# Moving the first w_down burst one pair of w_up tiles forward and pausing three times instead of twice

## The chip, the cores and the metric

The kernel runs on one core of a Trainium2 chip. The metric is the device time in microseconds of one execution, as a median over runs. The engines are named as in the profile: PE (matmuls), PEld (PE's weight loads), DVE (VectorE), ACT (ScalarE), POOL (GpSimd), SP (the engine that issues most of the DMAs).

## The reference: what is computed

One decoder layer on 256 positions of 1024 channels, float32. A first half (three kinds of attention, gates, an output projection and a residual) is followed by the gated channel mixer, which is where the change lies:

```python
    x = x + merged @ w_o

    h2 = rmsnorm(x, ln2)
    u = causal_dwconv(h2 @ w_up, conv_w, conv_b)
    a, b = jnp.split(u, 2, axis=-1)
    return x + (jax.nn.silu(a) * b) @ w_down
```

Here h2 is 256 x 1024, w_up is 1024 x 5632 (two halves of 2816 columns, for a and b), the convolution reaches over three positions per channel, and w_down is 2816 x 1024. A last rmsnorm follows. The inner width of 2816 is 22 blocks of 128 (NF = 22).

## The kernel before

**Weights.** All weights come as a stream of pieces of 128 x 1024 floats, in the order in which PE uses them. Each piece is loaded by SP into one of five `raw` buffers, ACT copies it in a rounded form to `whi` (line 113), and DVE subtracts the two to get the rest, `wlo` (line 120). A product is then three matmuls: hi by hi, hi by lo, lo by hi. `piece()` takes the next piece of the stream; `ahead()` prepares one more piece, some eight pieces ahead of the one in use. There are ten buffers each for `whi` and `wlo`.

**The channel mixer.** A loop over j = 0 to 21 makes one block of 128 inner channels at a time. It takes two pieces of w_up: `up(j, 0, u[0])` for the a half and `up(j, 1, u[1])` for the b half, 24 matmuls of 256 columns each, into the PSUM tiles called s (two of them, for even j) or pt and o (for odd j). In this document u0, u1, u2 are these pairs of w_up tiles. The matmuls read `h2T`, which has the name oT in the profile. `conv_of` takes a tile from PSUM to DVE (`v`, line 838), does the convolution on ACT and DVE (lines 841 to 845) and calls `ahead()` once. Silu and a product give `pr` (line 908); ACT rounds it to `ah` (line 914), DVE makes the rest `al` (line 915). These two are what w_down multiplies, and they have six buffers.

**The w_down bursts.** A row block d of w_down is one piece, and `down(d, parts)` is a burst of 12 matmuls of 512 columns, whose stationary operands are `ah` and `al` of block d. In this document d0, d1, ... are these bursts. A list decides after which pair which burst comes: `downs_after()` gives for each j a burst or none, and in the list the bursts go in order. The last four blocks (TAIL = 4) come after the loop. The stream of pieces in DRAM is laid out from the same list, so each piece still comes in the order of its use.

```python
        d = downs[j]
        if d is not None:
            parts = piece(0)
            ahead()
        nc.scalar.activation(hi, pr, AF.Copy)
        nc.vector.tensor_sub(lo, pr, hi.bitcast(F32))
        mid[j] = (hi, lo)
        if d is not None:
            down(d, parts)
```

So in a pair j with a burst, DVE and ACT prepare three pieces, and otherwise two. On DVE and ACT the third one stands between `pr` and `ah`, `al` of the same j. Engines run their own instructions strictly in the order in which the code issues them, and wait for each other by semaphores.

**Before u0.** The second rmsnorm needs the sum of squares of the whole x. Its factor goes to all partitions as `row2`, by matmuls (line 290) in the middle of u0 and a copy on ACT. Every `v` multiplies by `row2`, so DVE cannot begin with u0's tiles before that.

Of the kernel before, what the change touches and what calls it, by code (L numbers as in the profile page):

```python
# [37 lines left out]
          fours=(37.46, 53.0, 68.5, 83.5), mm=18.0)  # L38
DL = dict(pos=1.0, sq0=0.5, sq1=0.53, rs=1.0, row=1.0, q=1.98, g1=0.47, g2=0.64, s1=1.0, s2=1.43,
          s3=1.0, b=0.8, qk=1.9, half=2.0, ex=2.6, sc=1.3, fl=1.2, va=1.9, vh=0.9)  # L40
PAUSES = (9, 16)


def downs_after():

    out, d = [], 0
    for j in range(NF):
        if j >= 2 and j not in PAUSES:
            out.append(d)
            d += 1  # L50
        else:
            out.append(None)
    assert d == NF - TAIL
    return out
# [89 lines left out]
def hybrid_kernel(ctx: ExitStack, tc: tile.TileContext, x, head, ln_f, w_main, w_v1, w_v2, table,  # L144
# [742 lines left out]
    for r in (64, 0):  # L887
# [4 lines left out]
        if r:  # L892
            ml.tile([P, 48], F32, name="gap")

    downs = downs_after()
    for j in range(NF):
        u = up_banks(j)
# [164 lines left out]
```

## Time and profile before

| | |
|---|---|
| median of 3 runs | 382.51 us (382.28 to 382.6) |
| the profiled execution's own time | 381.96 us |
| its span in the trace | 380.2 us |
| PE busy | 372.1 us (98%) |
| DVE busy | 287.7 us (76%) |
| ACT busy | 230.3 us (61%) |
| granted clock of TensorE, mean | 0.997 |

The span runs from the first to the last instruction of the program; the execution's own time has some 1.8 us around it. Busy times are those of instructions that the engine works on. Matmuls are pipelined, and the duration of one overlaps the next, so the distance between two starts is their pace.

### The profile page before, as it was taken

Reading aid. Unit: us, or ns where it says so; the run is one execution under the profiler, and the core shown is the slowest. Engines: PE = TensorE matmul, PEld = TensorE weight load, DVE = VectorE, ACT = ScalarE, POOL = GpSimd, SP = SyncE. Lnnn points to the kernel's source line nnn. Section 1 sums busy time; section 2 is a strip of 40 time slices with the busy share of each in tenths; the row PEclk is TensorE's granted clock in tenths of the full one; section 3 lists DMA queues with packets and bytes.
Section 4 is the critical chain, followed back from the end, with each engine's and each line's share of the span. In section 5 each row is a group of like instructions: output and inputs, shape, how many; then the busy total and the mean of one; then the engine's idle time right before and its main releaser. Section 6 shows DMA issues by size and latency. Waiting matters only on the chain.

```text
span 380.2 us, 6522 instructions
## 1 busy us (share of the span) xinstructions
PE 372.1 (98%) x2470; PEld 334.6 (88%) x2470; DVE 287.7 (76%) x541; ACT 230.3 (61%) x398; POOL 5.0 (1%) x15
## 2 busy tenths in 40 slices
PE   8999999999999999999999999999999999999992
PEld 8999998787878788888899999999999999999982
DVE  4687876575757537967788999888987888888745
ACT  5875574547647694337587667556655656565433
POOL 1020000000000000000000000000000000000000
PEclk9999999999999999999999999999999999999998
DMA  7989964443442627435636567665566555563002
GB/s 254 400 286 345 334 187 167 139 159 132 166 165 90 218 92 267 161 117 166 243 98 233 203 218 238 208 208 181 174 216 193 197 183 205 171 218 110 2 0 110
DMA packets 20530, 70.86 MB, mean 186 GB/s; under 512 B 2278, under 2 KB 2708, under 8 KB 20500
## 3 DMA queue, kind: packets, MB, share of 16 engines
q1 hardware_dynamic: 19764, 68.11, 52.9%
q0 software_dynamic: 592, 2.12, 1.7%
q8 instruction: 19, 0.31, 0.3%
q10 hardware_dynamic: 144, 0.23, 0.2%
q14 instruction: 11, 0.09, 0.1%
HBM read 69.38 MB, written 1.07 MB: 185 GB/s over the span
## 4 chain that ended last, share of the span: by engine, by line
PE 96%; DMA 1%; DVE 1%; ACT 0%; SPq 0%; issue 0%; DVEq 0%
PE acc L244 16%; PE s L833 16%; PE acc L246 16%; PE acc L245 16%; PE pt L833 8%; PE o L833 8%; PE acc L390 7%; PE s L618 2%; DMA begin<-in_head 1%; PE pt L390 1%; PE o L390 1%; PE s L565 1%; PE s L607 1%; PE s L302 0%; PE pt L565 0%; PE pt L772 0%
## 5 line engine op out<-in xcount | busy, mean ns | idle before, releaser
L120 DVE TENSOR_TENSOR wlo<-raw,whi 128x1024 fp32r<-128x1024 f32 (+3 forms) x122 | 144.8, 1201 | 14.2 <-ACT whi L113 14.1
L113 ACT ACTIVATE whi<-raw 128x1024 fp32r<-128x1024 f32 (+3 forms) x122 | 124.1, 1038 | 42.8 <-PE acc L245 20.6
L833 PE MATMUL s<-oT,whi 128*128 128x256 f32 x352 | 62.5, 278 | 0.0
L244 PE MATMUL acc<-whi,hThi 128*128 128x512 f32 (+2 forms) x160 | 61.4, 384 | 0.0
L245 PE MATMUL acc<-whi,hTlo 128*128 128x512 f32 (+2 forms) x160 | 59.9, 374 | 0.0
L246 PE MATMUL acc<-wlo,hThi 128*128 128x512 f32 (+2 forms) x160 | 59.8, 374 | 0.0
L833 PEld LDWEIGHTS s<-oT,whi 128*128 128x128 f32 x352 | 54.1, 188 | 0.4
L833 PE MATMUL s<-oT,wlo 128*128 128x256 f32 x176 | 48.7, 277 | 0.0
L841 ACT ACTIVATE ya<-v,cv 128x256 f32<-128x256 f32 x22 | 13.3, 602 | 41.5 <-DVE v L838 41.5
L244 PEld LDWEIGHTS acc<-whi,hThi 128*128 128x128 f32 x160 | 30.0, 188 | 6.1 <-issue 1.3
L246 PEld LDWEIGHTS acc<-wlo,hThi 128*128 128x128 f32 x160 | 30.0, 188 | 5.2
L245 PEld LDWEIGHTS acc<-whi,hTlo 128*128 128x128 f32 x160 | 30.1, 188 | 4.7 <-DVE hTlo L296 0.2
L246 PE MATMUL acc<-wlo,ah 128*128 128x512 f32 (+1 forms) x88 | 34.1, 388 | 0.0
L244 PE MATMUL acc<-whi,ah 128*128 128x512 f32 (+1 forms) x88 | 34.0, 387 | 0.0
L245 PE MATMUL acc<-whi,al 128*128 128x512 f32 (+1 forms) x88 | 33.9, 385 | 0.0
L833 PEld LDWEIGHTS s<-oT,wlo 128*128 128x128 f32 x176 | 33.2, 188 | 0.4
L833 PE MATMUL pt<-oT,whi 128*128 128x256 f32 x176 | 32.1, 278 | 0.0
L833 PE MATMUL o<-oT,whi 128*128 128x256 f32 x176 | 31.8, 277 | 0.0
L833 PEld LDWEIGHTS pt<-oT,whi 128*128 128x128 f32 x176 | 27.4, 188 | 0.4
L833 PEld LDWEIGHTS o<-oT,whi 128*128 128x128 f32 x176 | 27.3, 188 | 0.0
L833 PE MATMUL pt<-oT,wlo 128*128 128x256 f32 x88 | 24.4, 277 | 0.0
L833 PE MATMUL o<-oT,wlo 128*128 128x256 f32 x88 | 24.3, 276 | 0.0
(236 smaller groups left out, 635.9 us busy)
## 6 DMA issues: line engine op xcount, KB each, us to landing
raw<-in_w_main SPq DMA_DIRECT2D x115, 512.0 KB, 3.5
begin<-in_head SPq DMA_DIRECT2D x6, 384.0 KB, 6.5
raw<-in_w_v SPq DMA_DIRECT2D x4, 384.0 KB, 3.9
xt<-in_x SPq DMA_DIRECT2D x2, 512.0 KB, 8.1
G<-rowsd POOLq DMA_DIRECT2D x1, 1024.0 KB, 14.3
raw<-in_w_v SPq DMA_DIRECT2D x2, 390.0 KB, 8.0
out_y<-xt SPq DMA_DIRECT2D x2, 288.0 KB, 2.2
begin<-in_head SPq DMA_DIRECT2D x2, 256.0 KB, 3.6
```

The source lines that it names most:

```text
L113: self.nc.scalar.activation(self.parts[i][0][:, cs], self.raw[i][:, cs], AF.Copy)
L120: self.nc.vector.tensor_sub(lo[:, cs], self.raw[i][:, cs], hi[:, cs].bitcast(F32))
L244: nc.tensor.matmul(o, lh, rh, start=start, stop=False, **kw)
L245: nc.tensor.matmul(o, ll, rh, start=False, stop=False, **kw)
L246: nc.tensor.matmul(o, lh, rl, start=False, stop=stop, **kw)
L390: nc.tensor.matmul(o, w[:, kk, cs], hT[h][:, k, :], start=first, stop=last, skip_group_check=True)
L565: nc.tensor.matmul(sc[2 * i + e][:, lo:lo + m], q[h, qi, qs], k[h, ki, 0:m], start=True, stop=True)
L607: nc.tensor.transpose(pts[h][:, i * P:(i + 1) * P], L[:, h, i * P:(i + 1) * P], ident)
L618: nc.tensor.matmul(os[i][e * HD:(e + 1) * HD, cs], v[t][:, vi, e, :], p[:, S:ROWS] if t else p[:, 0:S], start=t == 0, stop=t == 1, **kw)
L833: nc.tensor.matmul(u, w, h2T[h][:, k, :], start=k == 0 and i == 0, stop=k == KD - 1 and i == 2)
L841: nc.scalar.activation(y, v, AF.Identity, scale=w[2], bias=w[3])
```

## The change

```diff
-PAUSES = (9, 16)
+PAUSES = (8, 13, 18)
...
-        if j >= 2 and j not in PAUSES:
+        if j >= 1 and j not in PAUSES:
             out.append(d)
             d += 1
```

Before, d0 follows u2, and the pairs 9 and 16 have no burst behind them: a burst stands two pairs behind its block up to j = 8, three up to j = 15 and four up to j = 21. Now d0 follows u1, and the pairs 8, 13 and 18 have none: a burst stands one pair behind its block up to j = 7, two up to j = 12, three up to j = 17 and four up to j = 21. There are 18 bursts in the loop in both.

On PE, from the last matmul of u1 on, this stood before (`o` is u1's second tile, `s_2230` and `s_2231` are u2, `ah_2145` and `al_2146` are block 0, so the rows of line 244 to 246 are d0, and `pt` is u3):

```order
L833 MATMUL o<-oT,whi 128x256
L833 MATMUL s_2230<-oT,whi 128x256 [waits DVE_49]
...
L833 MATMUL s_2231<-oT,whi 128x256 [waits DVE_49,Activation_49]
...
L244 MATMUL acc<-whi,ah_2145 128x512 [waits Activation_49]
L245 MATMUL acc<-whi,al_2146 128x512 [waits DVE_49]
L246 MATMUL acc<-wlo,ah_2145 128x512
...
L833 MATMUL pt<-oT,whi 128x256 [waits DVE_49]
```

At the same place PE now has this (`s_2252` and `s_2253` are u2, `ah_2226` and `al_2227` are block 1, so the last two rows begin d1):

```order
L833 MATMUL o<-oT,whi 128x256
L244 MATMUL acc<-whi,ah_2145 128x512 [waits Activation_49]
L245 MATMUL acc<-whi,al_2146 128x512 [waits DVE_49]
L246 MATMUL acc<-wlo,ah_2145 128x512
...
L833 MATMUL s_2252<-oT,whi 128x256
...
L833 MATMUL s_2253<-oT,whi 128x256
...
L244 MATMUL acc<-whi,ah_2226 128x512 [waits Activation_49]
L245 MATMUL acc<-whi,al_2227 128x512 [waits DVE_49]
```

The 12 matmuls of d0, the first of which waits for `ah` and the second for `al` of block 0, have moved ahead of the 48 of u2.

On DVE nothing moves up to `pr` of block 1. Behind it, this is the first place where the two differ (`v<-s_2230` is the first work on u2's tiles):

```order
 L845 SCALAR_TENSOR_TENSOR yb<-v,cv,yb 128x254
 L908 TENSOR_TENSOR pr<-ya,yb 128x256
+L120 TENSOR_TENSOR wlo<-raw,whi 128x1024
 L915 TENSOR_TENSOR al_2227<-pr,ah_2226 128x256
-L838 TENSOR_TENSOR v<-s_2230,row_2074 128x256
```

Pair 1 now has a burst, so a third `wlo` stands ahead of `al` of block 1. What makes `al` of block 0 stands ahead of this, in the same rows as before.

## Rows read from the trace of the kernel before

**Rows 1.** The page, parts 1 and 4: busy time of each engine; the chain that ended last

```profile
PE 372.1 (98%) x2470; PEld 334.6 (88%) x2470; DVE 287.7 (76%) x541; ACT 230.3 (61%) x398; POOL 5.0 (1%) x15
PE 96%; DMA 1%; DVE 1%; ACT 0%; SPq 0%; issue 0%; DVEq 0%
```

**Rows 2.** The waits of PE's matmuls, whole span: us in total, times, longest

```profile
PE s L212 <- DVE warm L209: 1.1, 1, 1.1
PE s L618 <- DVE nm L577: 0.2, 1, 0.2
```

**Rows 3.** The waits of all engines, 212 to 366 us

```profile
DVE v L838 <- PE s L833: 8.2, 14, 1.1
```

**Rows 4.** The chain that ended last, in order of time: start us, us, what

```profile
203.48 5.65 PE s L833 x48
...
220.12 5.47 PE s L833 x48
...
266.66 5.44 PE s L833 x48
```

**Rows 5.** Timeline of PE, u2 to d1: start us, us, instruction

```profile
203.32 0.28 PE L833 MATMUL s<-oT,whi 128*128 128x256 f32 x1
...
208.97 0.40 PE L244 MATMUL acc<-whi,ah 128*128 128x512 f32 x1
...
211.77 0.28 PE L833 MATMUL pt<-oT,whi 128*128 128x256 f32 x1
...
217.21 0.39 PE L244 MATMUL acc<-whi,ah 128*128 128x512 f32 x1
...
219.96 0.28 PE L833 MATMUL s<-oT,whi 128*128 128x256 f32 x1
```

**Rows 6.** Timeline of DVE, blocks 0 to 2; in brackets idle before, and releaser

```profile
204.57 0.43 DVE L908 TENSOR_TENSOR pr<-ya,yb 128x256 f32<-128x256 f32 x1
205.47 0.43 DVE L915 TENSOR_TENSOR al<-pr,ah 128x256 fp32r<-128x256 f32 x1 [0.48 <-ACT ah L914]
205.82 0.42 DVE L838 TENSOR_TENSOR v<-pt,row 128x256 f32<-128x256 f32 x1
...
210.69 0.43 DVE L908 TENSOR_TENSOR pr<-ya,yb 128x256 f32<-128x256 f32 x1
...
211.95 0.42 DVE L838 TENSOR_TENSOR v<-s,row 128x256 f32<-128x256 f32 x1
...
216.82 0.43 DVE L908 TENSOR_TENSOR pr<-ya,yb 128x256 f32<-128x256 f32 x1
217.17 1.22 DVE L120 TENSOR_TENSOR wlo<-raw,whi 128x1024 fp32r<-128x1024 f32 x1
218.30 0.42 DVE L915 TENSOR_TENSOR al<-pr,ah 128x256 fp32r<-128x256 f32 x1
218.64 0.42 DVE L838 TENSOR_TENSOR v<-pt,row 128x256 f32<-128x256 f32 x1
```

**Rows 7.** Timeline of ACT, block 0 and the third piece of pair 2

```profile
205.03 0.42 ACT L914 ACTIVATE ah<-pr 128x256 fp32r<-128x256 f32 x1 [0.92 <-DVE pr L908]
...
215.32 2.00 ACT L113 ACTIVATE whi<-raw 128x1024 fp32r<-128x1024 f32 x2
```

**Rows 8.** Timeline, 7.8 to 10 us: a DVE result that PE waits for

```profile
8.50 0.69 DVE L120 TENSOR_TENSOR wlo<-begin,whi 128x512 fp32r<-128x512 f32 x1
...
9.25 0.38 PE L390 MATMUL pt<-hThi,wlo 128*128 128x256 f32 x1
```

**Rows 9.** The page, part 6: DMA issues of the weights, KB each, us to landing

```profile
raw<-in_w_main SPq DMA_DIRECT2D x115, 512.0 KB, 3.5
```

**Rows 10.** Timeline of PE: the first matmuls, eight of the same shape, the last matmul

```profile
1.10 3.35 PE L212 MATMUL s<-warm 128*128 128x128 f32 x14 [1.10 <-DVE warm L209]
...
172.49 1.03 PE L302 MATMUL s<-ident,G 128*128 128x128 f32 x8
...
373.21 0.28 PE L246 MATMUL s<-wlo,ah 128*128 128x256 f32 x1
```

**Rows 11.** Windows at the end: us, busy us of PE, PEld, DVE, ACT, POOL, PEclk, DMA share, GB/s

```profile
377.00:378.00 1.00, 0.00 (x0) 0.00 (x0) 0.00 (x0) 0.00 (x0) 0.00 (x0) 1.00 0.81 315
378.00:379.00 1.00, 0.00 (x0) 0.00 (x0) 0.00 (x0) 0.00 (x0) 0.00 (x0) 0.50 0.56 210
```

## The prediction, made before the changed kernel ran

> **What bounds the kernel now.** I read the page first. PE is busy for 98% of the span, and the chain that ended last is PE for 96% of it [rows 1]. So the time is PE's queue from end to end, and an edit costs or gains what it does to that queue. The next question is whether PE waits anywhere. The view of waits, asked for PE alone, has two entries over the whole span, 1.1 us at the start and 0.2 us in the attention part [rows 2]. In the channel mixer, where the change lies, there is none: PE goes from tile to tile without a gap, and it is DVE that waits there for PE, 14 times for the s tiles alone [rows 3].
>
> What is left are differences in PE's pace, which the chain in order of time shows. A pair of w_up tiles (48 matmuls) takes 5.65 us in u2, but 5.47 us later where a burst stands ahead of it, and 5.44 us behind a pair without a burst [rows 4]. The timeline of PE gives the bursts: d0 runs from 208.97 to 211.77, 2.80 us; d1 from 217.21 to 219.96, 2.75 us; between them u3 takes 5.44 us [rows 5]. So up to d0's end PE runs at a slightly slower pace, and from u3 on at the faster one. The trace does not say why; it shows that the switch came at the first change from a burst of 512 columns to w_up.
>
> The third view is the timeline of DVE and ACT at the place to which d0 moves. There DVE is far behind PE. PE leaves u1 and starts u2 at 203.32 [rows 5]. At that time `pr` of block 0 is not made yet: DVE makes it at 204.57, ACT `ah` from 205.03 to 205.45, DVE `al` from 205.47 to 205.90 [rows 6, 7]. The order of before hides this lag behind u2, 5.65 us of PE work. That is the point on which the prediction turns.
>
> **The change part by part.**
>
> *d0 behind u1.* PE reaches d0 at 203.32. Its first matmul needs `ah` of block 0, its second `al`. All that leads to these two stands in the same order on DVE and ACT as before, so their times hold. From the end of a DVE result to the matmul that waits for it I take 0.06 us: the `wlo` that began at 8.50 and took 0.69 us ended at 9.19, the matmul started at 9.25 [rows 8]. So the first matmul starts at about 205.45 + 0.06 = 205.51, and the second at 205.90 + 0.06 = 205.96, since its result is later than the first matmul needs. From the second on, 11 starts at 2.75 / 12 = 0.229 us bring d0's end to 205.96 + 2.52 = 208.48. The wait itself is 203.32 to 205.51, plus some 0.2 us between the first and the second matmul: about 2.4 us. The nearest row for the release is one of three in the trace's first microseconds; nothing for the release would make the sum smaller by 0.06.
>
> *What the pause gives back.* If the faster pace comes with the first burst, u2 takes 5.47 instead of 5.65 and d1 2.75, and u3, which now follows a burst, 5.47. The end of d1 and u3 together: 208.48 + 5.47 + 2.75 + 5.47 = 222.17. Before, the same four blocks (u2, d0, u3, d1) ended at 219.96 [rows 5]. That is +2.21 us. If the slow pace stays until d1 is over, d0 ends at 205.96 + 11 x 0.233 = 208.53, and with 5.65, 2.80 and 5.44 the four end at 222.42, +2.46 us. Of the two I take the faster pace, because the one switch in the trace came at the first burst; the other is the upper end.
>
> *d1 and later bursts, one pair behind their block.* In pair 1 a third `whi` and `wlo` now stand ahead of `al` of block 1. From `pr` to the end of `al` a pair with a third piece takes 218.30 + 0.42 - 216.82 = 1.90 us; ACT's two `whi` in such a pair (2.00 us) begin well ahead of `pr` [rows 6, 7]. `pr` of block 1 stands at 210.69, so `al` of block 1 is ready at 212.59. PE reaches d1 at 208.48 + 5.47 = 213.95, so there is a margin of 1.3 us. From then on it grows: DVE takes 218.64 - 211.95 = 6.69 us for a pair with three pieces [rows 6], PE takes 5.47 + 2.75 = 8.22. Cost nothing; if DVE lost more than 1.3 us in pair 1, PE would wait for the excess.
>
> *Three pauses instead of two, at other places.* In a pair without a burst PE needs 5.44 us and DVE 211.95 - 205.82 = 6.13 us [rows 4, 6], so DVE falls back by 0.7 us in each, and makes up 8.22 - 6.69 = 1.5 us in the next pair with a burst. Behind each pause a burst stands one pair further from its block, which is more room than the 0.7 us. The cover is the time in which DVE waits for PE [rows 3]; without it, 0.7 us per pause, and even that is smaller than the pair of room. Cost nothing. The changes from a burst to w_up, each 0.03 us (5.47 against 5.44), are 17 instead of 16; two of the 17 are in the sum above, so -0.03 remains against the 16 of before.
>
> *The pieces' order.* As many pieces, 115 loads of 512 KB, land in 3.5 us each [rows 9]. The fifth piece of the mixer's stream, once u2's first, is now w_down's first block. It is wanted at 203.32, as the fifth was before, and the next ones later than before, so preparation that was in time stays so. Cost nothing.
>
> *What a pause may do to PE's clock.* The last matmul of the program starts at 373.21, and the granted clock is still 1.00 in the window from 377 to 378, where no engine has an instruction; in the next window it is 0.50 [rows 10, 11]. The new wait is shorter than that stretch, so I add nothing. The Trainium skill, "TensorE: Matmul & The Clock Gate", section "HAM oscillation — how this bites in real kernels", says that a wait in which PE idles can throttle it and make the next matmuls run cold; by the rows of this case the sum gains nothing by that, by the rule, where it applied, it would gain about 1.6 us (the third rival works this out from rows).
>
> *Sum.* +2.21 - 0.03 = +2.2 us on PE, which has no later wait that could absorb it [rows 2]. The profiled execution took 381.96, which gives 384.2 for it; the median of the runs is 0.55 above the profiled one, 382.51 + 2.2 = **384.7 us**. Of no change a measurement of this kernel can tell about 0.2%, 0.77 us, so this would be slower, by 0.6%.
>
> **The rivals.**
>
> *First, not slower: no wait at d0.* If `al` of block 0 were ready at about 203.5, only the pace would change: u2 5.47 instead of 5.65, d0 2.75 instead of 2.80, together -0.23, 382.3 us. It decides at 203.5 + 0.06: `al` would have to come 2.4 us earlier than its row shows. For it speaks that DVE sat idle 0.48 us just ahead of `al`, and that a chain with three engines need not fall the same each time. Against it: what is ahead of `al` is untouched, and the idle time is far smaller than 2.4 us [rows 6]. That the burst doesn't move is excluded by the order on PE. Chance 0.05, of which 0.01 for faster by over 0.2%.
>
> *Second, d1 waits too.* The third piece in pair 1 comes late, because its raw load or its buffers are not free in time when DVE and ACT ask for it one pair earlier. The price beyond the margin: one `whi` and one `wlo` in a row (1.0 + 1.2 us [rows 6, 7]) less the margin of 1.3, so 0.9 us, 385.6 us; less if only part of it is late. For it: the third piece is the one that is new at this place. Against it: landing takes 3.5 us, and raw buffers run five pieces ahead. Chance 0.06.
>
> *Third, the clock falls in the wait.* The first 14 matmuls of the program, 128 columns each, took 3.35 us, eight of the same shape later 1.03 [rows 10], so at full pace the 14 would have taken 1.8 us: a start from rest cost some 1.6 us. If the wait for `ah` cost that again, it gives 384.7 + 1.6 = 386.3 us. Against it stand the windows at the end. It decides at a granted clock below 1.00 behind 203 us. Chance 0.04. It is the case that the page named above warns of.
>
> **How the numbers follow.** The forecast has a chance of 0.85. Its own bounds are +2.1 to +2.5 us, with the spread of the three runs around their median (-0.23, +0.09) 384.4 to 385.1. The second rival's smaller cases and a release that takes longer lie above this, up to 385.5; below, a DVE chain that is 0.2 us quicker gives 384.2. The range of **384.2 to 385.5** leaves out the first and the third rival and the far end of the second. Faster 0.01, same 0.04, slower 0.95.
>
> **What would show it.** In the profile of the changed kernel PE's waits should have a new entry at line 244 or 245 (or at their weight loads), released by ACT `ah` and DVE `al`, 2 to 2.5 us in all, near 203.3; `al` of block 0 should end at about 205.9 as before; u2 should take 5.47 us; d1 should start without a wait near 214; from there on every block should stand about 2.2 us later than before, with the same lengths, to the end. The prediction is wrong if `al` of block 0 comes earlier than its row here shows, if PE makes up time behind d1, or if u2 and d1 wait.

## The result and the profile after

The changed kernel takes 384.84 us (median of 5 executions, 384.8 to 386.74) against 382.28 us (median of 5, 382.14 to 382.6) in the same measurement. The ratio is 1.0075 with a 95% interval of 1.0063 to 1.0087: slower by 2.4 to 3.3 us. The profiled execution took 384.83 us, with a span of 383.1 us.

The page of the changed kernel, parts 1, 2 and 4: busy time of each engine, PE over the span in 40 slices, and the chain that ended last. They answer to [rows 1].

```profile
PE 372.0 (97%) x2470; PEld 333.9 (87%) x2470; DVE 288.1 (75%) x541; ACT 230.7 (60%) x398; POOL 5.0 (1%) x15
...
PE   7999999999999999999997999999999999999992
...
PE 94%; DVE 2%; DMA 1%; ACT 1%; issue 0%; SPq 0%; DVEq 0%
```

PE's busy time is that of before (372.0 against 372.1 us), and its share has fallen: the added time is time in which PE has nothing to do. The chain passes through DVE and ACT for a stretch. The slice of PE with a 7 in mid-span is from 201 to 211 us.

The waits of PE's matmuls over the whole span, which answer to [rows 2] (us in total, times, longest):

```profile
PE acc L244 <- ACT ah L914: 2.0, 1, 2.0
PE s L212 <- DVE warm L209: 1.1, 1, 1.1
PE pt L390 <- ACT whi L113: 0.5, 1, 0.5
PE o L390 <- ACT whi L113: 0.3, 1, 0.3
PE pt L390 <- DVE wlo L120: 0.2, 1, 0.2
PE s L618 <- DVE nm L577: 0.2, 1, 0.2
```

The first row is new and is the wait of d0 for `ah` of block 0. The three rows of line 390 lie in the first microseconds of the program, at the first weights; they belong to how this one execution began, and will be needed below to read the other times.

Timeline of PE at the end of u1, in d0 and at the start of u2, d1, u3 and d2, which answers to [rows 5]:

```profile
203.80 0.28 PE L833 MATMUL o<-oT,whi 128*128 128x256 f32 x1
206.09 0.49 PE L244 MATMUL acc<-whi,ah 128*128 128x512 f32 x1 [2.01 <-ACT ah L914]
206.55 0.50 PE L245 MATMUL acc<-whi,al 128*128 128x512 f32 x1
206.88 0.39 PE L246 MATMUL acc<-wlo,ah 128*128 128x512 f32 x1
...
209.18 0.28 PE L833 MATMUL s<-oT,whi 128*128 128x256 f32 x1
...
214.64 0.39 PE L244 MATMUL acc<-whi,ah 128*128 128x512 f32 x1
...
217.39 0.28 PE L833 MATMUL pt<-oT,whi 128*128 128x256 f32 x1
...
222.85 0.39 PE L244 MATMUL acc<-whi,ah 128*128 128x512 f32 x1
```

And that of DVE, which answers to [rows 6]:

```profile
205.16 0.42 DVE L908 TENSOR_TENSOR pr<-ya,yb 128x256 f32<-128x256 f32 x1
206.07 0.43 DVE L915 TENSOR_TENSOR al<-pr,ah 128x256 fp32r<-128x256 f32 x1 [0.48 <-ACT ah L914]
...
212.77 0.42 DVE L915 TENSOR_TENSOR al<-pr,ah 128x256 fp32r<-128x256 f32 x1
```

`pr` and `al` of block 0 stand 0.59 and 0.60 us later than in [rows 6], with the same distance between them. So this execution is 0.60 us late before the change has any effect (0.62 us at the first matmul of line 244: 18.88 against 18.26 before), and 0.60 is to be taken off every time here. The last u1 matmul starts at 203.80, the first of d0 at 206.09, the second, which needs `al`, at 206.55. d0 is over at 209.18; u2 takes 5.46 us, and d1 starts at 214.64, without a wait: `al` of block 1 ended at 213.19.

Last, the end of PE's work, which answers to [rows 10]:

```profile
376.08 0.28 PE L246 MATMUL s<-wlo,ah 128*128 128x256 f32 x1
```

That is 2.87 us later than the 373.21 of before. Without the 0.60 of the start it is 2.27 us. Nearly the same stands at the end of u3, where u2, d0, u3 and d1 are all done: 222.85 less 0.60, against 219.96 before, is 2.29 us.

### The profile page after: what moved, and what is told of

Its sections match the earlier page's. It is cut to its first block, busy times and chain, and to the rows that moved or that the text cites. A ratio compares the mean times of both kernels' runs of the same rounds, so it can differ in the third digit from the quotient of the medians.

```text
span 383.1 us, 6510 instructions
## 1 busy us (share of the span) xinstructions
PE 372.0 (97%) x2470; PEld 333.9 (87%) x2470; DVE 288.1 (75%) x541; ACT 230.7 (60%) x398; POOL 5.0 (1%) x15
## 4 chain that ended last, share of the span: by engine, by line
PE 94%; DVE 2%; DMA 1%; ACT 1%; issue 0%; SPq 0%; DVEq 0%
PE acc L244 16%; PE s L833 16%; PE acc L245 15%; PE acc L246 15%; PE pt L833 7%; PE o L833 7%; PE acc L390 7%; PE s L618 2%; DMA begin<-in_head 1%; PE pt L390 1%; PE o L390 1%; PE s L565 1%; PE s L607 1%; DVE wlo L120 0%; PE s L302 0%; PE pt L565 0%
```

## The experiments

Each was measured beside the kernel before on the same chip, in three series: the first with the four runs up to the shorter wait, the second with the two repeats, the first filling and the first delay of `al`, the third with the rest. The three series ran on three chips. With each run stands the number of timed executions.

**Is it the move or the pauses?** The move alone keeps d0 behind u1, and then pauses at pair 2, after which list and lags are those of before:

```diff
-PAUSES = (8, 13, 18)
+PAUSES = (2, 9, 16)
```

> d0 behind u1 as in the change, then a pause at pair 2 and the pauses at 9 and 16 of before: the move alone. Theory (the wait for block 0 at d0 is the whole cost): PE waits some 2.3 us at d0, +2.2 to +2.3 us from there, about 384.5 to 384.8 us, as the change. Rival (the pauses at other places, or the bursts one pair behind their blocks later on, carry a part): clearly less than the change, down to 382.3 us.

Measured: 386.28 us (5 executions, 386.04 to 386.85) against 382.39 of before (29 executions), ratio 1.0093 (1.0075 to 1.0111). This is slower than the change itself, and neither the theory nor the rival had expected that. The profile has the same wait of 2.01 us. But d0 took 4.44 us from its first matmul (205.96) to that of u2 (210.40), where it took 3.09 in the profile of the change, and the windows show why (columns as in [rows 11]):

```profile
204.00:205.00 1.00, 0.00 (x0) 0.00 (x0) 0.96 (x3) 0.57 (x1) 0.00 (x0) 1.00 0.74 291
205.00:206.00 1.00, 0.04 (x1) 0.04 (x1) 0.48 (x3) 0.42 (x1) 0.00 (x0) 0.96 0.83 229
206.00:207.00 1.00, 1.00 (x2) 0.75 (x3) 1.00 (x3) 0.26 (x1) 0.00 (x0) 0.50 0.73 287
...
209.00:210.00 1.00, 1.00 (x5) 0.77 (x5) 1.00 (x2) 1.00 (x3) 0.00 (x0) 0.84 0.90 311
```

The granted clock fell to 0.50, 1.2 GHz, as the wait ended, and came back during 209 to 210 us. That is the third rival of the prediction, which had been given 0.04.

The pauses alone keep d0 behind u2, as before:

```diff
-PAUSES = (9, 16)
+PAUSES = (13, 18)
```

> d0 behind u2 as before, pauses at 13 and 18 instead of 9 and 16: bursts two pairs behind their blocks up to pair 12. Theory: PE waits nowhere in the mixer, the time of before, 382.1 to 382.6 us. Rival (the later pauses cost): above 382.8 us, with a wait of PE behind pair 13.

Measured: 382.37 us (12 executions) against 382.39, ratio 0.9998 (0.9986 to 1.001). PE has no wait in the mixer. These other places for the pauses cost nothing.

**Is it the wait?** Here d0 stands between the two tiles of u2, one tile later than in the change; the list is that of before (left out of this cut: the later d0 of pair 2 is taken away, and its piece is laid one tile earlier in the stream):

```diff
+        if j == 2:
+            down(0, piece(0))
         if j:
             up(j, 1, u[1])
...
```

> The list of before, but d0 stands between the two tiles of u2, one tile of PE work (2.8 us) later than in the change. Theory: PE gets there at about 206.2, al of block 0 is ready at 205.9, so no wait to speak of (0 to 0.2 us) and the time of before, 382.0 to 382.5 us; the faster pace begins one tile earlier, -0.1 us. Rival (an earlier d0 costs by the other order of pieces, or by a burst between two w_up tiles, not by the wait): 383 us or more.

Measured: 382.31 us (12 executions) against 382.39, ratio 0.9993 (0.9982 to 1.0003). PE's waits again have no entry in the mixer. So this earlier d0 costs nothing, nor does a burst between two tiles; in the change it is one tile too early. The timeline of PE shows the pace change with the burst:

```profile
203.94 0.28 PE L833 MATMUL s<-oT,whi 128*128 128x256 f32 x1
...
206.77 0.40 PE L244 MATMUL acc<-whi,ah 128*128 128x512 f32 x1
...
209.56 0.28 PE L833 MATMUL s<-oT,whi 128*128 128x256 f32 x1
...
212.29 0.28 PE L833 MATMUL pt<-oT,whi 128*128 128x256 f32 x1
```

u2's first tile, ahead of d0, takes 2.83 us, its second, behind it, 2.73.

Then a shorter wait: the change with one `ahead()`, so one `whi` and one `wlo`, moved from `up_first` to behind `al` of block 0.

```diff
         for f in finish:
             f()
-        ahead()
...
         nc.vector.tensor_sub(lo, pr, hi.bitcast(F32))
+        if j == 0:
+            ahead()
```

> The change, with the preparation of one piece (one whi, one wlo) moved from ahead of u0's first v to behind al of block 0. Theory: ah and al of block 0 come 0.9 to 1.0 us earlier, the wait shrinks by as much, and the time by as much: 383.8 to 384.0 us. Rival (the cost is not the wait for block 0): the time of the change, 384.8 us, or more.

Measured: 383.61 us (12 executions, 383.31 to 384.01) against 382.39, ratio 1.0026 (1.0016 to 1.0037). The wait in the profile is 0.95 us shorter, as expected. The time is 1.2 us less than that of the change in its first measurement, which is another series, and a little under the 383.8 that were expected at least; the traces, compared below, give 0.93. In all 12 executions the mean clock was 0.994 to 0.998:

```profile
205.16 0.50 PE L244 MATMUL acc<-whi,ah 128*128 128x512 f32 x1 [1.06 <-ACT ah L913]
```

**What does the clock add?** The changed kernel and the move alone were each run once more.

> The changed kernel once more. Theory (wait of 2.3 us, and in some executions the granted clock falls to 0.50 behind the wait, which costs 1.3 to 1.9 us more): most executions at 384.8 us, one in five or so near 386.5. Rival (the move alone is slower than the change for another reason, its pause at pair 2): all executions near 384.8 us.

> The move alone once more. Theory (wait plus clock): executions at two levels, about 384.7 us where the clock stays and 386.0 to 386.8 us where it falls. Rival (its pause at pair 2 costs by itself): all at 386.0 us or more, whatever the clock.

The change: 385.63 us (6 executions) against 382.31 of before (11 executions), ratio 1.0082 (1.0066 to 1.0099). Three executions with a mean granted clock of 0.990 to 0.991 took 385.87 to 386.41 us, three with 0.995 took 384.57 to 385.39 us. The move alone: 385.3 us (6 executions), ratio 1.0084 (1.0063 to 1.0105); three with 0.989 to 0.991 took 386.0 to 386.78 us, three with 0.995 to 0.996 took 384.25 to 384.6 us. So both kernels have the same two levels, and in its first measurement the change had one of five on the upper one (386.74 us, clock 0.991). The pause at pair 2 shows no cost; all five executions of the move alone in the first series had the clock down (0.990 to 0.992). Of the kernel before, none of 29, 11 and 15 executions in the three series had a mean clock below 0.994. Where there is no profile, the mean is all that is known of the clock. The 13 profiles bear it out: the four in which the clock falls behind the wait have a mean of 0.990, the other nine 0.995 to 0.998.

The profile of the changed kernel taken here is one of the upper level. Its timeline of PE:

```profile
205.61 0.73 PE L244 MATMUL acc<-whi,ah 128*128 128x512 f32 x1 [2.01 <-ACT ah L914]
206.14 0.73 PE L245 MATMUL acc<-whi,al 128*128 128x512 f32 x1
206.67 0.63 PE L246 MATMUL acc<-wlo,ah 128*128 128x512 f32 x1
207.09 0.63 PE L244 MATMUL acc<-whi,ah 128*128 128x512 f32 x1
...
210.10 0.28 PE L833 MATMUL s<-oT,whi 128*128 128x256 f32 x1
...
215.75 0.39 PE L244 MATMUL acc<-whi,ah 128*128 128x512 f32 x1
```

The distance between two starts is 0.43 us where it is 0.23 at the full clock. d0 takes 4.49 us instead of 3.09, u2 5.65 instead of 5.46. The same kernel, the same wait of 2.01 us: in one profile the clock stays at 1.00, in the other it falls. The window behind the wait, first in the first profile of the change, then in this one:

```profile
206.00:207.00 1.00, 0.91 (x3) 0.60 (x4) 0.93 (x3) 0.17 (x2) 0.00 (x0) 1.00 0.90 352
```

```profile
206.00:207.00 1.00, 1.00 (x3) 0.83 (x3) 1.00 (x3) 0.61 (x2) 0.00 (x0) 0.50 0.59 238
```

If it is PE's idling that lets the clock fall, work for PE inside the wait must hold it. The first trial used 16 matmuls of a zero tile ahead of d0 in the move alone; their result is not used.

```diff
+        if d == 0:
+            fill = bank("s0", P)
+            for _ in range(16):
+                nc.tensor.matmul(fill, warm, warm, start=True, stop=True)
         if d is not None:
             down(d, parts)
```

> The move alone, with 16 matmuls of 128 columns on a tile of zeros ahead of d0, whose result is not used: about 1.7 us of PE work inside the wait. Theory: the clock stays at 1.00 behind the wait in every execution, d0 starts when it did, 384.6 to 384.9 us. Rival (the extra time of the move alone has nothing to do with the idle time of PE): 386.0 us or more, as without the filling.

Measured: 385.87 us (4 executions, 385.2 to 386.03), ratio 1.0091 (1.0078 to 1.0104). This is above the 384.6 to 384.9 that were expected, because the filling was too long. Each of these float32 matmuls makes two records, and d0 starts only behind all 32:

```profile
204.05 3.73 PE L920 MATMUL s<-warm 128*128 128x128 f32 x32
207.53 0.48 PE L244 MATMUL acc<-whi,ah 128*128 128x512 f32 x1
```

That is 1.31 us later than the 206.22 of the second profile of the move alone, whose u1 ends at the same time; with the 384.25 to 384.6 us of the move alone at the full clock, that about accounts for the time. The mean clock was 0.994 to 0.995 in all four. The second trial, in the change, has `range(8)`.

> The change, with 8 matmuls on a tile of zeros ahead of d0, 1.75 us of PE work that fits inside the wait of 2.0 us and whose result is not used. Theory (wait of 2.3 us, and the clock falls in some executions because PE idles): d0 starts no later than in the change, the granted clock stays at 1.00 behind it in every execution, all executions at 384.2 to 385.0 us, none near 386. Rival (the slower executions of the change have another cause): they are there as before, 385.9 to 386.8 us in about half of them.

Measured: 384.72 us (5 executions, 384.42 to 384.88) against 382.41 of before (15 executions), ratio 1.0062 (1.0048 to 1.0076). No execution was near 386, and the mean clocks were 0.994 to 0.997. The change without the filling was not measured in this series. The timeline shows that the filling ends ahead of d0's release, so d0 still waits for block 0 and starts 2.29 us behind the last matmul of u1 (203.68), as in the change:

```profile
203.80 1.95 PE L920 MATMUL s<-warm 128*128 128x128 f32 x16
205.97 0.50 PE L244 MATMUL acc<-whi,ah 128*128 128x512 f32 x1 [0.23 <-ACT ah L914]
206.43 0.50 PE L245 MATMUL acc<-whi,al 128*128 128x512 f32 x1
```

And the window behind the wait:

```profile
206.00:207.00 1.00, 1.00 (x4) 0.65 (x5) 1.00 (x3) 0.26 (x1) 0.00 (x0) 1.00 0.65 242
```

**Does the time follow `al` of block 0?** One useless DVE operation ahead of `al` of block 0, in three kernels:

```diff
+        if j == 0:
+            for _ in range(1):
+                nc.vector.tensor_add(G[:, 0, 0, :], G[:, 0, 1, :], G[:, 0, 1, :])
         nc.vector.tensor_sub(lo, pr, hi.bitcast(F32))
```

> The change, with one more DVE operation on 128 x 1024 floats, of no use, ahead of al of block 0. DVE is idle there for 0.48 us, so al comes 0.65 to 0.7 us later. Theory: the second matmul of d0 waits as much longer, 385.5 us where the clock stays. Rival (the cost is not this wait): 384.8 us.

Measured: 386.62 us (6 executions, 384.78 to 388.31), ratio 1.0114 (1.0092 to 1.0137). Five of the six had a clock of 0.990 to 0.991, so the time mixes the two costs and does not decide. The one with 0.994 took 384.78, the rival's figure and not the theory's 385.5; one execution does not decide either, where the change at such a clock took 384.57 to 385.39. The slowest, 388.31, is not explained. The profile is one with the clock down.

> The change with the 8 matmuls and with the one more DVE operation ahead of al of block 0. Theory: the clock stays, the second matmul of d0 waits 0.65 us more for al, so 0.5 to 0.7 us above the change with the 8 matmuls alone. Rival: the same time as that.

Measured, with the clock held: 385.32 us (5 executions, 384.9 to 385.48), 0.60 us above the filled change in the same series; ratio to before 1.0077 (1.0065 to 1.009). In the timeline of PE the second matmul now has a wait of its own:

```profile
205.57 0.50 PE L244 MATMUL acc<-whi,ah 128*128 128x512 f32 x1 [0.23 <-ACT ah L914]
206.59 0.50 PE L245 MATMUL acc<-whi,al 128*128 128x512 f32 x1 [0.52 <-DVE al L918]
```

So the clock stayed up, by the mean, in all 14 executions with a filling. In the series of the first trial, which has four of them, it fell in 11 of the 18 executions that had the wait and no filling. The ten others ran on another chip, where nothing with the wait and without a filling was measured; so the remedy rests on the four for its comparison on the same chip.

> The kernel before, with one more DVE operation on 128 x 1024 floats, of no use, ahead of al of block 0. Theory: u2 hides it, al is ready at about 206.6 and wanted at 209.2, no change, 382.0 to 382.6 us. Rival (DVE is the bound there anyway): +0.7 us, 383.0 us.

Measured: 382.35 us (11 executions) against 382.41, ratio 0.9999 (0.999 to 1.0007). Behind u2 the same delay costs nothing. In its timeline `al` starts at 206.57 on DVE, and d0 on PE at 209.50:

```profile
206.57 0.42 DVE L918 TENSOR_TENSOR al<-pr,ah 128x256 fp32r<-128x256 f32 x1
```

```profile
209.50 0.40 PE L244 MATMUL acc<-whi,ah 128*128 128x512 f32 x1
```

## Why the prediction was right, and where it was not

**The wait at d0 was right, to 0.1 us.** Predicted starts of 205.51 and 205.96 are 205.49 and 205.95 in the profile once 0.60 is taken off, so the release of 0.06 us held. d0 ended at 208.58 instead of 208.48: the third matmul started 0.33 us behind the second instead of 0.229, which the sum did not have. That the wait is the cost is shown from both sides: take it away by one tile of PE work, and the time is that of before (ratio 0.9993); shorten it, and the time falls; delay `al`, and the time rises by 0.60 us in the filled change and by nothing in the kernel before. The traces show it without the differences between executions at their start. The stretch from the start of u1's last matmul to that of the program's last one compares as follows:

| kernel | stretch, us | against before |
|---|---|---|
| before (203.20 to 373.21) | 170.01 | |
| other pauses alone; before with `al` delayed | 170.01 | 0.00 |
| d0 one tile later | 169.90 | -0.11 |
| change, first profile (203.80 to 376.08); filled change | 172.28 | +2.27 |
| change with the wait 0.95 us shorter | 171.35 | +1.34 |
| filled change with `al` delayed | 172.86 | +2.85 |
| move alone with the longer filling | 173.34 | +3.33 |
| change with the clock down | 173.89 | +3.88 |
| move alone with the clock down, two profiles | 173.61, 173.82 | +3.60, +3.81 |
| change with `al` delayed, clock down | 174.01 | +4.00 |

**The pace was right.** u2 took 5.46 and d1 2.75 us behind the early d0. Why PE runs at 5.65 us per pair ahead of the first burst stays open. It is not always the first burst that ends it either: in the profile of the change with the clock down, u2 kept to 5.65 us and d1 ended it, but in the two of the move alone with the clock down u2 took 5.44 and 5.47 us.

**d1 without a wait, the pauses, the order of the pieces: right.** `al` of block 1 was ready 1.45 us ahead of d1, against the margin of 1.3 that was worked out, and the pauses alone measured 0.9998.

**The third rival was ruled out wrongly.** Its price of 1.6 us came out: beyond the +2.27 of the wait, the three profiles of the change and of the move alone with the clock down have 1.61, 1.33 and 1.54 us. In that of the change, d0 took 1.40 us more, u2 0.19 and d1 0.04. The agreement is in part luck. The price was that of the program's first 14 matmuls, but in the trace of before the slow pace goes on behind these, to 5.96 us, so a whole start cost more; and the granted clock stands at 1.00 in the windows there, so the rows don't show that the slow pace at the start is the clock's. The view merges them by two there; from one row to the next it is 0.42 us at first, then 0.23:

```profile
5.54 0.58 PE L390 MATMUL o<-hThi,whi 128*128 128x256 f32 x2
5.96 0.39 PE L390 MATMUL o<-hTlo,whi 128*128 128x256 f32 x2
6.19 0.39 PE L390 MATMUL o<-hThi,wlo 128*128 128x256 f32 x2
```

Its chance of 0.04 was wrong: the clock fell in 1 of 5 and 3 of 6 executions of the change, and in 5 of 5 and 3 of 6 of the move alone. The step that failed is the reading of [rows 10, 11], where the clock stayed at 1.00 for some four and a half microseconds behind the last matmul. That was one event in one execution, and it was taken for a bound. The ends of the traces alone show that it is none: over the 13 of this case, the clock fell from 2.2 to 4.9 us behind PE's last matmul. In the change's own profile PE's work ends at 376.36, and the clock falls in the first of these two windows:

```profile
379.00:380.00 1.00, 0.00 (x0) 0.00 (x0) 0.17 (x1) 0.32 (x1) 0.00 (x0) 0.86 0.19 71
380.00:381.00 1.00, 0.00 (x0) 0.00 (x0) 0.00 (x0) 0.00 (x0) 0.00 (x0) 0.50 0.91 361
```

In the mixer, in the four profiles of the table with the clock down, it fell 2.0 to 2.4 us behind the end of u1, so about when d0 began (0.04 us ahead of it in one profile, 0.10 to 0.41 us behind it in the three others). The Trainium skill, which the prediction named, says in "TensorE: Matmul & The Clock Gate", section "HAM oscillation — how this bites in real kernels", that a long enough wait, in which PE idles, throttles it and the next matmuls start cold. The traces agree in these executions, with 0.50 behind a wait of 2.01 us, and not in the others, with 1.00 behind the same wait; the gap that the page gives as the limit is longer than this wait, and the measurement decides. What decides between the executions is not settled by these runs.

**The size, and the luck in it.** The prediction had +2.2 us; the traces give 2.27 without the difference at the start, the medians 2.56. That the median of 384.84 lies so near the 384.7 is in part luck, since the kernel before stood at 382.28 in this measurement and not at the 382.51 from which the sum started. So is that it lies in the range: only one of the five executions had the clock down, and with three of six in the repeat the median was 385.63 us, above the range's 385.5. The filled change, which has the wait but not the clock, is 1.8 to 2.9 us above before (1.0048 to 1.0076), so the wait alone accounts for most of it. What is more in the change's own interval (2.4 to 3.3 us) fits the one execution of five with the clock down. The 0.60 us with which the profile after starts late is not of the change: PE's waits that go with it lie at the first weights, and the executions of before differ by more than that among themselves (381.95 to 384.13 over the 29 of the first series).

## What to carry to other kernels

A consumer can be moved forward at no cost only to the place where its producer is done: read when the operand's last instruction ends, compare it with the time at which the reader's engine would get there, and the difference is the cost, one to one, where that engine is the bound (here 0.95 us less wait gave 0.93 us). Other work to put in between is worth looking for at a finer grain than the loop's: here one w_up tile instead of two was enough to hide the lag, though it made the kernel no faster than before. And a wait on the matmul engine had a second price here, the clock behind it, which one profile may not show; the mean granted clock of every execution did.

## What was not expected of the hardware

An idle stretch of PE of 2.01 us, between two stretches of dense matmuls, was followed by a granted clock of 0.50 in 12 of 22 executions of the change and of the move alone (by their mean clock), with matmuls of 512 columns at 0.43 instead of 0.23 us. The same wait with 1.95 us of matmuls of zeros in it was not, in ten of ten, and an idle stretch of 1.06 us was not, in twelve of twelve. And at the full clock a burst that starts from a wait loses 0.1 us at its third matmul: 0.33 to 0.35 us behind the second instead of 0.23, in the change, the filled kernels and the shortened wait alike.
